# The last head of an mLSTM block: its z units ahead of its weighted values, and one weight split ahead of the squares

## The chip, the cores and the metric

The kernel runs on one core of one Trainium2 chip. The metric is the device time of one execution in microseconds (us); shorter is better. The core has five engines that run side by side, each in the order of its own instructions: TensorE (PE in the profile; its loads of weights are PEld), VectorE (DVE), ScalarE (ACT), GpSimd (POOL), and SyncE (SP), which here only issues DMAs.

## The reference

The block has one layer, 512 positions and 1024 channels. A combined projection gives a Fourier branch (a) and an mLSTM branch (b) of 2048 channels in 4 heads of 512; both are gated, mapped back to 1024 channels, merged and projected once more. What matters here is the end of branch b:

```python
h_cell = h_cell * jax.nn.sigmoid(o_m)                       # per head: 512 positions x 512 channels
h_cell = h_cell * lax.rsqrt(jnp.mean(h_cell * h_cell, axis=-1, keepdims=True) + EPS)
y_b = ((h_cell * hnorm_w[l] + skip_w[l] * x_c) * jax.nn.silu(z_m)) @ w_mlstm[l]
```

## The kernel before

**Split numbers.** Every fp32 weight and activation that TensorE reads is split into a high and a low part: ACT writes the high part (`hi_of`, L90), DVE subtracts it from the source (`lo_of`, L93). A product is three matmuls (`mm3`, L97 high by high, L98 the activation's low part, L99 the weight's low part).

**Weight units.** Weights come in units of 128x1024, fetched by SP into `raw` (3 buffers) and split by `prepare` into `whi` and `wlo` (2 buffers each). `unit()` hands out the oldest split unit and keeps two split ahead in the program's text. A DMA of a new unit is issued with each `prepare`.

**A head.** The loop over `h` makes scores, decay weights and the output gate `so`. Then, for four row tiles t of 128 positions: the weighted values `pv` (12 matmuls in a `wk` bank), `so *= pv` on DVE (L684), the sum of squares on ACT (L686), its root on POOL (L688, L689), and the scaling of `so` on DVE (L690). Then 16 transposes on PE (L700, four per row tile, into one `wk` bank per channel tile d), and for each d on DVE the norm weight and skip (L702), the gate by `sz[d]` (L703), and the split into `u_hi` (tiles `sa`, ACT) and `u_lo` (tiles `sb`, DVE). The four z units of a head (`z_unit`) give `sz`; from the second head on, unit 0 stands ahead of the row tiles and units 1 to 3 behind them.

**Branch b's product.** `u` times `w_mlstm` runs over 16 weight units in two halves of eight. In the first half, units 0 to 3 need `u` of the first two heads alone, units 4 and 5 that of the third, units 6 and 7 that of the last. After units 6 and 7 ACT copies the four sums out (L751). Inside this half lie two calls of `block_sums` for a later stage: POOL fetches `xr`, DVE makes sums `xs` and the low parts `bl` and `tl`, ACT the high parts `bh` and `th`.

**Order.** The text is not the order in which an engine runs. A scheduler in the framework builds one list per engine by a timeline of its own before the kernel runs; `pin` (`keep_in_program_order`) keeps an instruction in the text's order among the pinned ones of its engine. On the chip each engine works off its list strictly in order.

Of the kernel before, what the change touches and what calls it, by code (L numbers as in the profile page):

```python
# [10 lines left out]
AF = mybir.ActivationFunctionType  # L11
ALU = mybir.AluOpType
# [5 lines left out]
NH = 4  # L18
# [7 lines left out]
NU0 = 3  # L26
# [14 lines left out]
def hybrid_block(ctx: ExitStack, tc, xT, x0n, xn, first, units, blocks, vecs, gates, gbias, consts, dft, fnw, out):  # L41
    nc = tc.nc
    te, ve, se, gp = nc.tensor, nc.vector, nc.scalar, nc.gpsimd
# [21 lines left out]
    def tl(tag, shape, dtype=F32, bufs=1, pool=None, shift=0):  # L65
        count[0] += 1
        if pool is None:
            pool = "wide" if tag[:2] in ("sa", "sb") else "gw" if tag in ("gwh", "gwl") else "low" if tag in LOW else "high" if tag in HIGH else "work"


        n = math.prod(shape[1:])
        t = pools[pool][1].tile([shape[0], -(-(n + shift) // 64) * 64], dtype, tag=tag, name=f"{tag}_{count[0]}", bufs=bufs)
        t = t[:, shift : shift + n]
        if len(shape) == 2:
            return t
        names = "abcd"[: len(shape) - 1]
        return t.rearrange(f"p ({' '.join(names)}) -> p {' '.join(names)}", **dict(zip(names, shape[1:])))

    def bank(tag, cols=512, rows=P):
        count[0] += 1  # L80
        return ps.tile([rows, cols], F32, tag=tag, name=f"{tag}_{count[0]}", bufs=4)

    def t2k(dtype=F32, cols=S):
        return tl("t2k", [P, cols], dtype, bufs=3)

    def pin(ins, on=True):
        return tc.keep_in_program_order(ins) if on else ins

    def hi_of(dst, src, scale=1.0, pinned=False):
        pin(se.activation(dst, src, AF.Copy, scale=scale), pinned)  # L90

    def lo_of(dst, src, hi, pinned=False):
        pin(ve.tensor_tensor(out=dst, in0=src, in1=hi.bitcast(F32), op=ALU.subtract), pinned)  # L93

    def mm3(acc, wh, wl, xh, xl, start, stop, pinned=False, group=True):
        skip = {} if group else {"skip_group_check": True}
        pin(te.matmul(acc, wh, xh, start=start, stop=False, **skip), pinned)  # L97
        te.matmul(acc, wh, xl, start=False, stop=False, **skip)  # L98
        te.matmul(acc, wl, xh, start=False, stop=stop, **skip)  # L99
# [25 lines left out]
    def fetch():  # L125
        i = state["raw"]
        if i < nplan:
            raws[i] = tl("raw", [P, 1024], bufs=NRAW)
            if len(plan[i]) == 1:
                w = plan[i][0].shape[1]  # L130
                pin(nc.sync.dma_start(raws[i][:, 0:w], plan[i][0]))
            else:
                for n, src in enumerate(plan[i]):
                    pin(nc.sync.dma_start(raws[i][:, n * S : (n + 1) * S], src))
            state["raw"] += 1

    def raw_unit(i):
        while state["raw"] <= i:
            fetch()
        return raws.pop(i)  # L140

    def prepare():
        i = state["split"]
        r = raw_unit(i)
        extra = i >= first_pair and i % 4 >= 2
        hi = tl("gwh" if extra else "whi", [P, 1024], F32R, bufs=2)
        lo = tl("gwl" if extra else "wlo", [P, 1024], F32R, bufs=2)
        w = 1024 if len(plan[i]) == 2 else plan[i][0].shape[1]
        hi_of(hi[:, 0:w], r[:, 0:w], pinned=i <= NU0 + 2)
        lo_of(lo[:, 0:w], r[:, 0:w], hi[:, 0:w], pinned=i <= NU0 + 2)  # L150
        items.append((hi, lo))
        state["split"] += 1
        fetch()
# [16 lines left out]
    def unit():  # L170
        i = state["split"]
        if state["at"] < len(JOBS) and i >= JOBS[state["at"]]:
            state["at"] += 1
            next_job()
        while len(items) < (4 if "gw" in pools else 2) and state["split"] < nplan:
            prepare()
        return items.pop(0)
# [21 lines left out]
    def col(o):  # L199
        return vc[:, o : o + 1]  # L200
# [46 lines left out]
    for g in range(2):  # L247
        part = []
        for k in range(4):
            sq = tl(f"{('sa', 'sb')[g]}{k}", [P, S])  # L250
# [92 lines left out]
    def first_units():  # L343
        accs = [bank(t) for t in ("acc", "wk", "acc")]
        for n in range(4):
            for i, ((wh, wl), acc) in enumerate(zip(firsts, accs)):
                last = n == 3 and i == 2
                if last:
                    load_gates()
                    prepare()  # L350
                    prepare()
                for k in (2 * n, 2 * n + 1):
                    if last and k == 7:
                        norm_rows()
                    ks = slice(k * P, (k + 1) * P)
                    mm3(acc, wh[:, ks], wl[:, ks], hv(x_hi, k), hv(x_lo, k), k == 0, k == 7, last)
        return accs

    def proj(hooks={}, pinned=False):
        wh, wl = unit()  # L360
        acc = bank("acc")
        for k in range(8):
            if k in hooks:
                hooks[k]()
            ks = slice(k * P, (k + 1) * P)
            mm3(acc, wh[:, ks], wl[:, ks], hv(x_hi, k), hv(x_lo, k), k == 0, k == 7, pinned or any(at <= k for at in hooks))
        return acc

    def evac(dst, acc, func=None, pinned=False):
        pin(ve.tensor_tensor(out=dst, in0=acc, in1=rb, op=ALU.mult), pinned)  # L370
        if func:
            se.activation(dst, dst, func)
# [3 lines left out]
    def new_sz():  # L376
        z2 = [tl(f"sz{n}", [P, 2, S]) for n in range(2)]
        sz.extend(z2[n // 2][:, n % 2, :] for n in range(4))

    def z_unit(d, func=AF.Silu):  # L380
        if not sz:
            new_sz()
        evac(sz[d], proj(), func)
# [42 lines left out]
    def spread_rows(h):  # L426
        for dr in range(2):
            r = 32 * dr + h
            spread[dr] = tl(("mx_r", "em_r")[dr], [P, S])
            pin(nc.sync.dma_start(spread[dr], kept_rows[0][r : r + 1, :].to_broadcast([P, S])))  # L430
        spread[2] = tl("em", [P, S], bufs=2)
        for dr in range(2):
            r = 32 * dr + h
            pin(nc.sync.dma_start(spread[2][64 * dr : 64 * dr + 64], kept_rows[1][r : r + 1, :].to_broadcast([64, S])))
# [58 lines left out]
    for h in range(NH):  # L493
# [100 lines left out]
        so = [so2[t // 2][:, t % 2, :] for t in range(4)]  # L594

        def o_gate():
            for t in range(4):
                se.activation(so[t], ops[t], AF.Sigmoid, scale=rc[:, t : t + 1])
# [42 lines left out]
        r = t2k()  # L641
# [31 lines left out]
        if h < NH - 1:  # L673
            spread_rows(h + 1)
        o_gate()
        if h > 0:
            z_unit(0)
        ss = tl("ss", [P, 4], bufs=2)
        for t in range(4):
            pv = bank("wk")  # L680
            for b in range(4):
                o = (t if t <= b else t + 1) * P
                mm3(pv, whi[b][:, o : o + P], wlo[b][:, o : o + P], vh[b], vl[b], b == 0, b == 3)
            ve.tensor_tensor(out=so[t], in0=pv, in1=so[t], op=ALU.mult)  # L684
            sq = t2k()
            se.activation(sq, so[t], AF.Square, accum_out=ss[:, t : t + 1])  # L686
            r = tl("rr", [P, 1], bufs=4)
            gp.tensor_scalar(out=r, in0=ss[:, t : t + 1], scalar1=1.0 / 512, scalar2=EPS, op0=ALU.mult, op1=ALU.add)  # L688
            gp.tensor_tensor(out=r, in0=r, in1=mhalf, op=ALU.pow)  # L689
            ve.tensor_scalar(out=so[t], in0=so[t], scalar1=r, scalar2=None, op0=ALU.mult)  # L690
        for d in range(4):
            if h > 0 and d > 0:
                z_unit(d)
            c = c0 + d
            se.activation(xc[c], xc[c], AF.Copy, scale=col(V_SK + c))
# [256 lines left out]
    def m_split(key, src):  # L952
        shape = [src.shape[0]] + list(src.shape[1:])
        hi, lo = (tl(f"m{key[0]}{x}{key[1]}", shape, F32R, pool="last") for x in "hl")
        hi_of(hi, src)
        lo_of(lo, src, hi)
        return hi, lo

    mb, mt = {}, {}
    for j in range(8):  # L960
# [19 lines left out]
        else:  # L980
            k = j - 4
            hi, lo = m_split(("c", k), ga)
# [7 lines left out]
            hi, lo = m_split(("d", k), ts)  # L990
# [209 lines left out]
```

## Time and profile before

| | us |
|---|---|
| median of 3 runs | 753.75 (753.0 to 755.37) |
| the profiled execution | 753.18 |
| its span in the trace | 751.4 |
| PE busy in it | 741.6 (99%) |
| DVE, ACT, POOL busy | 529.1, 410.8, 68.0 |

The profiled execution is 0.57 us below the median, and 1.8 us of it lie outside the span. All rows below are of that one execution. A row of a timeline gives the start, the length, the engine, the line with what it writes and reads, and in brackets how long the engine had been idle and what ended that. An instruction's length holds its way through the engine, so that the next one can start before it ends; the step from start to start is what one costs its engine.

### The profile page before, as it was taken

Reading aid. Unit: us, or ns where it says so; the run is one execution under the profiler, and the core shown is the slowest. Engines: PE = TensorE matmul, PEld = TensorE weight load, DVE = VectorE, ACT = ScalarE, POOL = GpSimd, SP = SyncE. Lnnn points to the kernel's source line nnn. Section 1 sums busy time; section 2 is a strip of 40 time slices with the busy share of each in tenths; the row PEclk is TensorE's granted clock in tenths of the full one; section 3 lists DMA queues with packets and bytes.
Section 4 is the critical chain, followed back from the end, with each engine's and each line's share of the span. In section 5 each row is a group of like instructions: output and inputs, shape, how many; then the busy total and the mean of one; then the engine's idle time right before and its main releaser. Section 6 shows DMA issues by size and latency. Waiting matters only on the chain.

```text
span 751.4 us, 10918 instructions
## 1 busy us (share of the span) xinstructions
PE 741.6 (99%) x4127; PEld 640.2 (85%) x4127; DVE 529.1 (70%) x833; ACT 410.8 (55%) x639; POOL 68.0 (9%) x142
## 2 busy tenths in 40 slices
PE   9999999999999999999999999999999999999996
PEld 8888876888888888888888778899999999988885
DVE  6999985785758574757566866257667787556976
ACT  7345465677626772668343443266544587543444
POOL 0001000204100210022100410000010100000002
PEclk9999999999999999999999999999999999999999
DMA  8548865385945489255720794267654466555463
GB/s 293 179 146 232 236 226 140 92 286 134 240 132 223 114 218 298 87 176 132 196 84 29 190 286 137 88 200 220 192 162 151 148 170 196 168 183 152 141 195 115
DMA packets 42243, 131.24 MB, mean 175 GB/s; under 512 B 4880, under 2 KB 5648, under 8 KB 37072
## 3 DMA queue, kind: packets, MB, share of 16 engines
q1 hardware_dynamic: 38288, 106.84, 42.9%
q0 software_dynamic: 3616, 23.33, 15.4%
q8 instruction: 32, 0.52, 0.3%
q10 hardware_dynamic: 288, 0.39, 0.1%
q14 instruction: 19, 0.16, 0.1%
HBM read 128.19 MB, written 44.30 MB: 230 GB/s over the span
## 4 chain that ended last, share of the span: by engine, by line
PE 97%; ACT 1%; DVE 1%; POOL 0%; issue 0%; ACTq 0%; POOLq 0%
PE acc L97 17%; PE acc L99 17%; PE acc L98 17%; PE wk L97 8%; PE wk L98 8%; PE wk L99 8%; PE acc L585 4%; PE acc L584 4%; PE acc L583 4%; PE wk L666 2%; PE acc L1046 1%; PE acc L1048 1%; PE acc L1047 1%; PE wk L304 1%; PE wk L700 1%; PE wk L197 1%
## 5 line engine op out<-in xcount | busy, mean ns | idle before, releaser
L90 ACT ACTIVATE whi<-raw 128x1024 fp32r<-128x1024 f32 (+2 forms) x107 | 108.4, 1018 | 118.1 <-PE acc L98 68.1
L93 DVE TENSOR_TENSOR wlo<-raw,whi 128x1024 fp32r<-128x1024 f32 (+2 forms) x107 | 124.8, 1171 | 66.4 <-ACT whi L90 66.4
L97 PE MATMUL acc<-hhi,whi 128*128 128x512 f32 x240 | 94.6, 394 | 0.0
L98 PE MATMUL acc<-hlo,whi 128*128 128x512 f32 x240 | 93.5, 390 | 0.0
L99 PE MATMUL acc<-hhi,wlo 128*128 128x512 f32 x240 | 93.4, 389 | 0.0
L93 DVE TENSOR_TENSOR gwl<-raw,gwh 128x1024 fp32r<-128x1024 f32 (+1 forms) x39 | 47.1, 1209 | 18.3 <-ACT gwh L90 18.3
L90 ACT ACTIVATE gwh<-raw 128x1024 fp32r<-128x1024 f32 (+1 forms) x39 | 40.9, 1049 | 29.0 <-PE acc L98 10.0
L97 PEld LDWEIGHTS acc<-hhi,whi 128*128 128x128 f32 x240 | 45.2, 188 | 9.5 <-issue 0.2
L98 PEld LDWEIGHTS acc<-hlo,whi 128*128 128x128 f32 x240 | 45.2, 188 | 9.4 <-issue 0.2
L99 PEld LDWEIGHTS acc<-hhi,wlo 128*128 128x128 f32 x240 | 45.0, 188 | 9.4
L584 PE MATMUL acc<-wlo,hhi 128*128 128x512 f32 x128 | 50.5, 395 | 0.0
L585 PE MATMUL acc<-whi,hlo 128*128 128x512 f32 x128 | 50.4, 394 | 0.0
L97 PE MATMUL acc<-sa,whi 128*128 128x512 f32 x128 | 49.3, 392 | 0.9 <-ACT whi L90 0.9
L99 PE MATMUL acc<-sa,wlo 128*128 128x512 f32 x128 | 48.9, 391 | 1.1 <-DVE wlo L93 1.1
L98 PE MATMUL acc<-sb,whi 128*128 128x512 f32 x128 | 49.7, 391 | 0.0
L97 PE MATMUL wk<-vhi,phi 128*128 128x512 f32 x128 | 49.6, 389 | 0.0
L98 PE MATMUL wk<-vlo,phi 128*128 128x512 f32 x128 | 49.6, 389 | 0.0
L99 PE MATMUL wk<-vhi,plo 128*128 128x512 f32 x128 | 48.5, 389 | 0.0
L583 PE MATMUL acc<-whi,hhi 128*128 128x512 f32 x128 | 47.0, 394 | 0.0
L333 DVE SCALAR_TENSOR_TENSOR t2k<-sa,vecs,t2k 128x510 f32<-128x510 f32 (+1 forms) x64 | 44.9, 744 | 0.1
L93 DVE TENSOR_TENSOR vlo<-wk,vhi 128x512 fp32r<-128x512 f32 x32 | 21.0, 682 | 27.5 <-ACT vhi L90 27.5
L99 PEld LDWEIGHTS acc<-sa,wlo 128*128 128x128 f32 x128 | 24.0, 188 | 6.8 <-DVE wlo L93 1.9
(427 smaller groups left out, 1904.1 us busy)
## 6 DMA issues: line engine op xcount, KB each, us to landing
raw<-in_units_dram SPq DMA_DIRECT2D x69, 512.0 KB, 4.2
sum<-in_blocks_dram SPq DMA_DIRECT2D x20, 1024.0 KB, 8.0
raw<-sum SPq DMA_DIRECT2D x64, 256.0 KB, 3.7
raw<-in_blocks_dram SPq DMA_DIRECT2D x48, 256.0 KB, 3.8
sum<-in_blocks_dram POOLq DMA_DIRECT2D x10, 1024.0 KB, 9.7
sum<-sum POOLq DMA_DIRECT2D x10, 1024.0 KB, 9.4
raw<-sum SPq DMA_DIRECT2D x8, 512.0 KB, 4.4
raw<-in_blocks_dram SPq DMA_DIRECT2D x6, 512.0 KB, 4.6
```

The costliest lines, as they stand in the source:

```text
L90: pin(se.activation(dst, src, AF.Copy, scale=scale), pinned)
L93: pin(ve.tensor_tensor(out=dst, in0=src, in1=hi.bitcast(F32), op=ALU.subtract), pinned)
L97: pin(te.matmul(acc, wh, xh, start=start, stop=False, **skip), pinned)
L98: te.matmul(acc, wh, xl, start=False, stop=False, **skip)
L99: te.matmul(acc, wl, xh, start=False, stop=stop, **skip)
L197: te.matmul(junk[:, 0:P], ones, ones, start=True, stop=True)
L304: pin(te.matmul(gate_ps[rows, :], w_gate[j][:, i, :], r, start=n == 0, stop=n == 14, tile_position=(0, 32 * (2 * b + j))), n + b + j > 0)
L333: ve.scalar_tensor_tensor(out=cv[:, o], in0=src[:, s], scalar=cw[k], in1=cv[:, o], op0=ALU.mult, op1=ALU.add)
L583: te.matmul(ops[t], hv(x_hi, k)[:, ts], wh[:, ks], start=k == 0, stop=False)
L584: te.matmul(ops[t], hv(x_hi, k)[:, ts], wl[:, ks], start=False, stop=False)
L585: te.matmul(ops[t], hv(x_lo, k)[:, ts], wh[:, ks], start=False, stop=k == 7)
L666: te.matmul(vp[:, ds], xm[c0 + d][:, b * P : (b + 1) * P], vbf[:, d, :], start=True, stop=True)
```

## The change

In the last head alone, all four z units stand ahead of the row tiles; behind them one `prepare` is called, with its two split instructions pinned; and the products with `pv` and the squares of the four row tiles are pinned too.

```diff
-    def prepare():
+    def prepare(ahead=False):
...
-        hi_of(hi[:, 0:w], r[:, 0:w], pinned=i <= NU0 + 2)
-        lo_of(lo[:, 0:w], r[:, 0:w], hi[:, 0:w], pinned=i <= NU0 + 2)
+        hi_of(hi[:, 0:w], r[:, 0:w], pinned=ahead or i <= NU0 + 2)
+        lo_of(lo[:, 0:w], r[:, 0:w], hi[:, 0:w], pinned=ahead or i <= NU0 + 2)
...
+        last = h == NH - 1
         if h > 0:
-            z_unit(0)
+            for d in range(4 if last else 1):
+                z_unit(d)
+        if last:
+            prepare(True)
         ss = tl("ss", [P, 4], bufs=2)
         for t in range(4):
...
-            ve.tensor_tensor(out=so[t], in0=pv, in1=so[t], op=ALU.mult)
+            pin(ve.tensor_tensor(out=so[t], in0=pv, in1=so[t], op=ALU.mult), last)
             sq = t2k()
-            se.activation(sq, so[t], AF.Square, accum_out=ss[:, t : t + 1])
+            pin(se.activation(sq, so[t], AF.Square, accum_out=ss[:, t : t + 1]), last)
...
         for d in range(4):
-            if h > 0 and d > 0:
+            if 0 < h < NH - 1 and d > 0:
                 z_unit(d)
```

Lines behind L676 move down by four: L684 and L686 become L688 and L690, L690 becomes L694, L700 to L703 become L704 to L707, L723 to L728 become L727 to L732.

What this makes of the lists is seen at three places. **Place 1** is ACT at the row tiles of the last head. `whi_3692` is the high part of branch b's unit 3, `whi_3738` that of unit 4, `phi` are the decay weights that `pv` reads. Before:

```order
L648 ACTIVATE plo_633_3204<-t2k_3199 64x512 x2
L90 ACTIVATE phi_634_3236<-wf_601_3019 128x640
L90 ACTIVATE phi_636_3243<-wf_602_3020 128x640
L90 ACTIVATE phi_638_3250<-wf_603_3021 128x640
L90 ACTIVATE phi_640_3257<-wf_604_3022 128x640
L686 ACTIVATE t2k_3383,ss_3368<-so_616_3127 128x512
L686 ACTIVATE t2k_3403,ss_3368<-so_616_3127 128x512
L686 ACTIVATE t2k_3423,ss_3368<-so_617_3128 128x512
L686 ACTIVATE t2k_3443,ss_3368<-so_617_3128 128x512
L90 ACTIVATE whi_3692<-raw_3634 128x1024
L90 ACTIVATE whi_3738<-raw_3664 128x1024
L90 ACTIVATE bh_712_3618<-xr_3722 128x256
```

After:

```order
L648 ACTIVATE plo_633_3204<-t2k_3199 64x512 x2
L90 ACTIVATE whi_3692<-raw_3471 128x1024
L90 ACTIVATE phi_634_3236<-wf_601_3019 128x640
L90 ACTIVATE phi_636_3243<-wf_602_3020 128x640
L90 ACTIVATE phi_638_3250<-wf_603_3021 128x640
L90 ACTIVATE phi_640_3257<-wf_604_3022 128x640
L690 ACTIVATE t2k_3488,ss_3473<-so_616_3127 128x512
L690 ACTIVATE t2k_3508,ss_3473<-so_616_3127 128x512
L690 ACTIVATE t2k_3528,ss_3473<-so_617_3128 128x512
L690 ACTIVATE t2k_3548,ss_3473<-so_617_3128 128x512
L90 ACTIVATE whi_3738<-raw_3664 128x1024
L90 ACTIVATE bh_715_3624<-xr_3722 128x256
```

The split of unit 3 moved from behind the last square to ahead of the decay weights; that of unit 4 is still behind the last square. Of the 24 matmuls of unit 3, which before all stood behind the first 12 transposes, PE's list now has 16 ahead of the 48 weighted values and 8 among those transposes. The 48 themselves, which took turns over the four row tiles, now go almost tile by tile.

On DVE, at the same place, `wk_3369` to `wk_3429` were the weighted values of row tiles 0 to 3. Before:

```order
L684 TENSOR_TENSOR so_616_3127<-wk_3369,so_616_3127 128x512
L684 TENSOR_TENSOR so_616_3127<-wk_3389,so_616_3127 128x512
L690 TENSOR_SCALAR so_616_3127<-so_616_3127,rr_3385 128x512
L684 TENSOR_TENSOR so_617_3128<-wk_3409,so_617_3128 128x512
L690 TENSOR_SCALAR so_616_3127<-so_616_3127,rr_3405 128x512
L684 TENSOR_TENSOR so_617_3128<-wk_3429,so_617_3128 128x512
L690 TENSOR_SCALAR so_617_3128<-so_617_3128,rr_3425 128x512
L93 TENSOR_TENSOR wlo_3693<-raw_3634,whi_3692 128x1024
```

After, where they are `wk_3474` to `wk_3534`:

```order
L688 TENSOR_TENSOR so_616_3127<-wk_3474,so_616_3127 128x512
L694 TENSOR_SCALAR so_616_3127<-so_616_3127,rr_3490 128x512
L688 TENSOR_TENSOR so_616_3127<-wk_3494,so_616_3127 128x512
L694 TENSOR_SCALAR so_616_3127<-so_616_3127,rr_3510 128x512
L688 TENSOR_TENSOR so_617_3128<-wk_3514,so_617_3128 128x512
L694 TENSOR_SCALAR so_617_3128<-so_617_3128,rr_3530 128x512
L688 TENSOR_TENSOR so_617_3128<-wk_3534,so_617_3128 128x512
L93 TENSOR_TENSOR wlo_3739<-raw_3664,whi_3738 128x1024
```

Each product with `pv` now stands behind the scaling of the tile before it; before, one product stood between.

**Place 2** is PE at the four transposes of row tile 3, the last ones. Before (`acc_3629` is unit 3, `acc_3626` with `whi_3738` the first of unit 4):

```order
L98 MATMUL acc_3629<-sb_446_2312,whi_3692 128x512
L99 MATMUL acc_3629<-sa_445_2311,wlo_3693 128x512
L97 MATMUL acc_3626<-sa_563_2921,whi_3738 128x512
L700 MATMUL wk_3552<-consts_192,so_617_3128 128x128
L700 MATMUL wk_3564<-consts_192,so_617_3128 128x128
L700 MATMUL wk_3576<-consts_192,so_617_3128 128x128
L700 MATMUL wk_3588<-consts_192,so_617_3128 128x128
L98 MATMUL acc_3626<-sb_564_2922,whi_3738 128x512
L99 MATMUL acc_3626<-sa_563_2921,wlo_3739 128x512
```

After (`acc_3633` with `whi_3738` ends unit 4, `acc_3634` begins unit 5):

```order
L98 MATMUL acc_3633<-sb_576_2958,whi_3738 128x512
L99 MATMUL acc_3633<-sa_575_2957,wlo_3739 128x512
L704 MATMUL wk_3558<-consts_192,so_617_3128 128x128
L704 MATMUL wk_3570<-consts_192,so_617_3128 128x128
L704 MATMUL wk_3582<-consts_192,so_617_3128 128x128
L704 MATMUL wk_3594<-consts_192,so_617_3128 128x128
L97 MATMUL acc_3634<-sa_563_2921,whi_3768 128x512
L98 MATMUL acc_3634<-sb_564_2922,whi_3768 128x512
```

The four transposes moved from behind unit 4's first matmul to behind its last. From them to the first matmul that reads `u` of the last head there were 47 matmuls; now there are 24.

**Place 3** is DVE behind those transposes, from the first L702 to the first `sb` of the last head (`sb_691_3561`, now `sb_694_3567`). Before, ten instructions stood ahead of it (one row counts for two):

```order
L702 SCALAR_TENSOR_TENSOR t2k_3557<-wk_3552,vecs_108,sb_138_768 128x512
L702 SCALAR_TENSOR_TENSOR t2k_3569<-wk_3564,vecs_108,sb_140_778 128x512
L702 SCALAR_TENSOR_TENSOR t2k_3581<-wk_3576,vecs_108,sb_142_786 128x512
L93 TENSOR_TENSOR tl_708_3614<-xs_3723,th_704_3610 128x1024
L703 TENSOR_TENSOR t2k_3557<-t2k_3557,sz_657_3331 128x512
L93 TENSOR_TENSOR wlo_3769<-raw_3696,whi_3768 128x1024
L703 TENSOR_TENSOR t2k_3569<-t2k_3569,sz_657_3331 128x512
L723 SCALAR_TENSOR_TENSOR xr_3798<-xr_3798,vecs_108,rb_235 128x512 x2
L703 TENSOR_TENSOR t2k_3581<-t2k_3581,sz_658_3332 128x512
L93 TENSOR_TENSOR sb_691_3561<-t2k_3557,sa_690_3560 128x512
```

After, seventeen do. The three L706, an `xr`, the low part of unit 6 and a second `xr` come first; these are the rest:

```order
L707 TENSOR_TENSOR t2k_3563<-t2k_3563,sz_657_3331 128x512
L727 SCALAR_TENSOR_TENSOR xr_3798<-xr_3798,vecs_108,rb_235 128x512
L707 TENSOR_TENSOR t2k_3575<-t2k_3575,sz_657_3331 128x512
L707 TENSOR_TENSOR t2k_3587<-t2k_3587,sz_658_3332 128x512
L730 TENSOR_TENSOR xs_3723<-xr_3722 128x256
L732 SCALAR_TENSOR_TENSOR xs_3723<-xs_3723,xr_3722 128x256
L93 TENSOR_TENSOR bl_719_3628<-xr_3722,bh_715_3624 128x512
L729 TENSOR_TENSOR xs_3799<-xr_3798 128x256
L93 TENSOR_TENSOR bl_720_3629<-xr_3798,bh_716_3625 128x256
L730 TENSOR_TENSOR xs_3799<-xr_3798 128x256
L93 TENSOR_TENSOR wlo_3845<-raw_3772,whi_3844 128x1024
L93 TENSOR_TENSOR sb_694_3567<-t2k_3563,sa_693_3566 128x512
```

The sums of `block_sums`, which stood ahead of the first L702 or behind the first `sb`, and the low part of unit 7 now lie between the two. On ACT the first `sa` of the last head, before one place behind the split of unit 5, now stands behind that of unit 7 (`whi_3844`).

PE's list is the same up to the first matmuls of branch b's unit 0, the 96 matmuls of the last head's z units among them. SP's list has the same kinds of rows in the same order.

## Rows read from the trace of the kernel before

**Rows 1.** The page: share of the chain that ended last, by engine.

```profile
PE 97%; ACT 1%; DVE 1%; POOL 0%; issue 0%; ACTq 0%; POOLq 0%
```

**Rows 2.** PE's own waits, whole span: us in total, times, longest us.

```profile
PE acc L99 <- DVE wlo L93: 1.1, 2, 0.5
PE acc L97 <- ACT whi L90: 0.9, 2, 0.7
```

**Rows 3.** Timeline of PE at the last head's transposes; start us, us, engine, line, operation.

```profile
415.39 0.39 PE L99 MATMUL wk<-vhi,plo 128*128 128x512 f32 x1
415.62 2.03 PE L700 MATMUL wk<-consts,so 128*128 128x128 f32 x12
418.32 0.50 PE L97 MATMUL acc<-sa,whi 128*128 128x512 f32 x1 [0.67 <-ACT whi L90]
...
419.58 0.50 PE L99 MATMUL acc<-sa,wlo 128*128 128x512 f32 x1 [0.53 <-DVE wlo L93]
419.92 0.39 PE L97 MATMUL acc<-sa,whi 128*128 128x512 f32 x1
```

**Rows 4.** Timeline of PE between the halves of branch b.

```profile
446.73 0.39 PE L99 MATMUL acc<-sa,wlo 128*128 128x512 f32 x1
...
448.99 0.39 PE L97 MATMUL acc<-sa,whi 128*128 128x512 f32 x1
```

**Rows 5.** Timeline of PE at the last four transposes.

```profile
424.02 0.39 PE L97 MATMUL acc<-sa,whi 128*128 128x512 f32 x1
...
424.70 0.39 PE L97 MATMUL acc<-sa,whi 128*128 128x512 f32 x1
424.94 0.60 PE L700 MATMUL wk<-consts,so 128*128 128x128 f32 x4
...
425.60 0.40 PE L99 MATMUL acc<-sa,wlo 128*128 128x512 f32 x1
```

**Rows 6.** Timeline of ACT at the squares of the last head.

```profile
416.60 0.63 ACT L686 ACTIVATE t2k<-so 128x512 f32<-128x512 f32 x1 [1.09 <-DVE so L684]
...
417.23 1.99 ACT L90 ACTIVATE whi<-raw 128x1024 fp32r<-128x1024 f32 x2
```

**Rows 7.** Timeline of DVE at the row tiles.

```profile
410.83 0.69 DVE L684 TENSOR_TENSOR so<-wk,so 128x512 f32<-128x512 f32 x1 [5.41 <-PE wk L99]
...
413.23 0.49 DVE L690 TENSOR_SCALAR so<-so,rr 128x512 f32<-128x512 f32 x1
...
415.82 0.69 DVE L684 TENSOR_TENSOR so<-wk,so 128x512 f32<-128x512 f32 x1 [0.52 <-PE wk L99]
...
418.30 1.23 DVE L93 TENSOR_TENSOR wlo<-raw,whi 128x1024 fp32r<-128x1024 f32 x1 [1.36 <-ACT whi L90]
```

**Rows 8.** Timeline of DVE from the first L702 of the last head on.

```profile
425.24 2.07 DVE L702 SCALAR_TENSOR_TENSOR t2k<-wk,vecs,sb 128x512 f32<-128x512 f32 x3
...
430.70 1.41 DVE L723 SCALAR_TENSOR_TENSOR xr<-xr,vecs,rb 128x512 f32<-128x512 f32 x2
...
432.63 0.68 DVE L93 TENSOR_TENSOR sb<-t2k,sa 128x512 fp32r<-128x512 f32 x1
433.23 1.22 DVE L93 TENSOR_TENSOR wlo<-raw,whi 128x1024 fp32r<-128x1024 f32 x1
...
437.84 0.42 DVE L728 SCALAR_TENSOR_TENSOR xs<-xs,xr 128x256 f32<-128x256 f32 x1
438.17 1.22 DVE L93 TENSOR_TENSOR wlo<-raw,whi 128x1024 fp32r<-128x1024 f32 x1
```

**Rows 9.** Timeline of POOL: the four fetches of `xr`.

```profile
416.53 2.31 POOL L722 DMA_DIRECT2D xr<-in_xT_dram  x4
```

**Rows 10.** All eight fetches of `xr`, from issue to landing.

```profile
DMA to landing us min/median/max: 3.3/4.0/13.3
```

**Rows 11.** Stretches: us, busy us (instructions) of PE, PEld, DVE, ACT, POOL, granted clock, DMA.

```profile
416.00:420.00 4.00, 2.67 (x14) 1.49 (x13) 2.30 (x4) 2.62 (x4) 3.73 (x7) 1.00 0.53 163
749.00:750.00 1.00, 0.00 (x0) 0.00 (x0) 0.00 (x0) 0.00 (x0) 0.00 (x0) 1.00 0.86 322
```

## The prediction

> **What bounds the kernel now.** I read the chain of waits first: 97% of it is PE [rows 1], so time is won or lost only where PE stands still. The list of PE's waits says how often that is: apart from the start, twice for a high part and twice for a low part of a weight unit [rows 2]. PE's timeline gives the places. The first is the end of the last head [rows 3]: from 415.62 to 419.92, 4.30 us, PE does 12 transposes and 3 matmuls. A matmul costs 0.227 us (424.02 to 424.70 are three), and four transposes cost 425.60 - 424.94 - 0.227 = 0.43, so 0.108 each [rows 5]. That is 1.30 + 0.68 of work; **2.32 us is standing still**. The second place lies between the halves of branch b [rows 4]: 446.73 to 448.99 holds four matmuls, 0.91 of 2.26 us, so 1.35 are lost. In both, PE waits for the split of the next weight unit, on ACT and then on DVE. The change touches the first place alone. Its most possible gain is thus 2.32 us, 0.31% of 753.75; about 0.3% is what a measurement of this kernel can tell from no change.
>
> **The z units and the pins.** PE's 96 matmuls of the last head's z units keep their place, so moving them in the text costs and gives PE nothing. The only trace is that the split of unit 1 comes a few places later on ACT and DVE. Were the unit not ready, the loss would be at most one split, 1.07 from high to low part [rows 6, 7] and 1.28 from there to PE [rows 3, 7]; at the least it is nothing. I take nothing, because unit 0's matmuls lie in front of it. The pins are not instructions and cost nothing by themselves; SP's list is unchanged, so no DMA is issued past another one.
>
> **The early split of unit 3: 2.32 us gained, part of it given back.** The split no longer waits behind the last square (416.60 and then 417.23 [rows 6]), so 16 of unit 3's matmuls can run ahead of the weighted values and 8 among the transposes. What is late next is unit 4, whose high part is still behind the last square. I follow that chain in the time of the trace of before.
> - PE: the last weighted value started at 415.39 [rows 3]; 16 matmuls more make it 415.39 + 3.63 = 419.02. Then come 12 transposes and 8 matmuls, so PE reaches unit 4 at 419.02 + 0.227 + 1.30 + 1.82 = 422.37.
> - DVE: a product with pv starts 0.43 after the last matmul's start (415.39 to 415.82 [rows 3, 7]), and its own scaling starts 2.40 later (410.83 to 413.23, by way of ACT and POOL [rows 7]) and costs 0.40 (0.49 long, and a step is 0.08 to 0.09 shorter than a length: 432.63 to 433.23 for 0.68 [rows 8]). Since each product now stands behind the scaling of the tile before it, four tiles are 2.80 apart, while PE delivers one every 12 x 0.227 = 2.72. Tile 0 ends 33 matmuls before the last one, at 411.53; so its product starts at 411.96 and tile 3's at 411.96 + 3 x 2.80 = 420.36, and not at 419.45, when PE would allow it.
> - ACT and on: square 0.78 later (415.82 to 416.60), high part 0.63 after that (to 417.23), PE 1.09 after that (to 418.32), low part 1.07 after the high part's start (to 418.30), its first matmul 1.28 after that (to 419.58; the 1.23 of its length and 0.05) [rows 3, 6, 7]. So the high part starts at 421.77, PE at 422.86, and the first matmul with the low part at 424.12.
>
> PE waits 0.49 for the first. Four matmuls run by the high part alone; the one behind a wait costs 0.34 instead of 0.227 (419.58 to 419.92 [rows 3]), so they end at 423.88 and PE waits 0.24 again. With 0.11 for each restart, **0.95 us is given back**.
>
> **The later transposes: a new wait.** The transposes of tile 3 follow unit 4's other 20 matmuls: 424.12 + 0.34 + 19 x 0.227 = 428.77. The first L706 follows 0.30 later (424.94 to 425.24 [rows 5, 8]), at 429.07; DVE has by then done the low parts of units 4 and 5, if `xr` has landed. It is fetched behind tile 2's root, at about 420; the issues take 2.31 and the quickest landing 3.3 [rows 9, 10], while DVE wants it at about 424.4.
>
> From here DVE has 17 instructions to do before the first low part of the last head's u. Their price comes from the stretch of before that holds almost the same ones without a pause, 425.24 to 438.17, 12.93 us [rows 8]. It has one L702 (0.66), one `tl` (1.13, the size of a `wlo`) and three `sb` (0.60 each) more, and one `xr` (0.66) and one `xs` (0.33) fewer: 12.93 - 0.66 - 1.13 - 1.80 + 0.66 + 0.33 = 10.33. The low part starts at 439.40, and PE can read it 0.73 later (its 0.68 and the same 0.05 as above), at 440.13.
>
> PE has 4 transposes and 24 matmuls to do meanwhile: it is done with unit 5 at 428.77 + 0.43 + 5.45 = 434.65. Two waits follow.
> - The first u's high part (`sa`) stands on ACT behind unit 7's split, which needs the buffer that unit 5's last matmul but one frees: 434.65 - 0.45 + 0.43 = 434.63 (a release at the price of rows 7). Its step is 0.95 (two are 1.99 long [rows 6]), and `sa` takes 0.63 and 0.05: PE starts at 436.26, a wait of 1.61.
> - Four matmuls read high parts alone, to 437.28. Then the low part is wanted, which comes at 440.13: 2.85 more.
>
> With two restarts this is **4.68 us lost**. It would vanish only if PE had other work there, and its list has none. The rest of u follows close on the first low part, with PE's next reads 32 matmuls on, so I add no third wait. The joint at 446 has the same rows in the same order and keeps its 1.35.
>
> **The sum.** -2.32 + 0.95 + 4.68 = +3.3 us. The profiled execution took 753.18, 0.57 below the median; it becomes 756.5, and the median 753.75 becomes **757.0**, 0.44% slower.
>
> **Rivals.**
> - *The gain without the new wait* (8%). For it speaks that the old wait does go. It needs u's low part by 437.28; DVE would have to do its 17 instructions in 7.5 us. It decides at a new loss of 2.32 - 0.95 = 1.37: below that the kernel is not slower. With none, 753.75 - 1.37 = 752.4. Against it stands a DVE without a pause in the very stretch.
> - *Half the new wait* (12%). The price of the 17 instructions is a sum of steps, and tile 3's transposes could come up to 0.95 sooner if unit 4 does not wait. With half of 4.68: 753.75 + 1.0 = 754.7.
> - *The xr fetch lands late* (6%). The longest of the eight landings is 13.3 [rows 10]. DVE stops at L727 and with it everything behind: from 424.4 to 433.3, of which the pause before 429.07 hides some 2; about 6 us more, 763. Against it: the four are issued close together and in the same place of POOL's list as before.
> - *The clock falls after the new wait* (4%). In a stretch with 1.33 of 4 us idle the granted clock was 1.00, the upper level of 2.4 GHz, and in 749 to 750, with PE idle throughout, it still was [rows 11]. At 1.2 GHz a matmul takes 0.45 instead of 0.227; for half of the 44 that are left of units 6 and 7 this is 5 us, 762. The Trainium skill, page "TensorE: Matmul & The Clock Gate", section "Why this matters for your kernels", asks to leave no long idle gaps between bursts of matmuls, since one sends the clock back to half; by that rule this change risks both losses. The trace disagrees so far as its own idle stretches go, none of which had matmuls behind it at half the clock.
> - *The change doesn't do what it says*: the split does stand ahead of the squares in ACT's list, so this has no chance of its own; of the z units it is true.
>
> **How the numbers follow.** The forecast has 70%; it spans some 0.8 us each way, since four terms are differences of starts rounded to 0.01 that rest on a single execution, and since runs of before differ by 2.4 us. The range takes in the half wait: 754.4 to 758.8, and leaves out the full gain, the late fetch and the clock. Slower by over 0.3% (above 756.0): nine tenths of the forecast's 70%, and the late fetch and the clock, 72%. Within 0.3%: the rest of the forecast, the half wait and most of the gain, 22%. Faster: 6%.
>
> **What would show it.** In the trace after: no PE wait at the first 12 transposes; a wait of about 0.5 for unit 4's high part and 0.2 for its low part; then, some 12 us later, waits of about 1.6 for `sa` on ACT and 2.8 for `sb` on DVE, with DVE busy throughout from the first L706; then 1.35 at the joint as before. It is wrong if PE waits for `sb` under 1.4 us in all, or if another wait, for `xr` or `raw`, stands there.

## The result, and the profile after

The median rose from 753.74 us to **758.66 us** (six executions each, 752.96 to 755.37 and 758.09 to 760.5): a ratio of 1.0067, with an interval of 1.0052 to 1.0082. The change costs 4.9 us. The profiled execution of the changed kernel took 760.5, its span is 758.7. It falls 1.4 us behind within its first 25 us, at its first loads and long before the change, and keeps that: its first product with `pv` starts at 413.40 where the prediction has 411.96. All times of this trace below stand 1.44 later than those of the prediction for that reason.

PE's waits now, whole span (us in total, times, longest us), against [rows 2]:

```profile
PE acc L97 <- ACT sa L90: 2.1, 1, 2.1
PE acc L98 <- DVE sb L93: 2.0, 1, 2.0
...
PE acc L97 <- ACT whi L90: 0.9, 3, 0.3
PE acc L99 <- DVE wlo L93: 0.5, 1, 0.5
```

Two waits of about 2 us that were not there before now lead the list, for the two halves of the last head's u. PE's timeline at the last head's transposes, against [rows 3] (start us, us, engine, line, operation; in brackets idle and releaser):

```profile
420.46 0.39 PE L99 MATMUL wk<-vhi,plo 128*128 128x512 f32 x1
420.69 0.27 PE L704 MATMUL wk<-consts,so 128*128 128x128 f32 x1
...
422.52 0.39 PE L99 MATMUL acc<-sa,wlo 128*128 128x512 f32 x1
422.75 1.25 PE L704 MATMUL wk<-consts,so 128*128 128x128 f32 x10
424.34 0.50 PE L97 MATMUL acc<-sa,whi 128*128 128x512 f32 x1 [0.33 <-ACT whi L90]
...
425.14 0.40 PE L98 MATMUL acc<-sb,whi 128*128 128x512 f32 x1
425.60 0.50 PE L99 MATMUL acc<-sa,wlo 128*128 128x512 f32 x1
```

The 2.32 us of standing still behind the last weighted value are gone. Instead unit 4 is waited for: 424.34 - 422.75 less ten transposes at 0.108 is 0.51, and 425.60 - 425.14 - 0.227 is 0.23. Ten microseconds on comes the large loss:

```profile
435.96 0.39 PE L99 MATMUL acc<-sa,wlo 128*128 128x512 f32 x1
438.45 1.20 PE L97 MATMUL acc<-sa,whi 128*128 128x512 f32 x4 [2.10 <-ACT sa L90]
441.64 0.80 PE L98 MATMUL acc<-sb,whi 128*128 128x512 f32 x1 [2.00 <-DVE sb L93]
442.24 0.63 PE L99 MATMUL acc<-sa,wlo 128*128 128x512 f32 x1
442.67 0.63 PE L97 MATMUL acc<-sa,whi 128*128 128x512 f32 x1
...
446.93 0.43 PE L98 MATMUL acc<-sb,whi 128*128 128x512 f32 x1
447.20 0.40 PE L99 MATMUL acc<-sa,wlo 128*128 128x512 f32 x1
```

From start to start PE loses 438.45 - 435.96 - 0.227 = 2.26 for `sa`. Four matmuls (0.91) later it loses 441.64 - 438.45 - 0.91 = 2.28 for `sb`, of which 0.11 is the restart behind the first wait and 2.17 the wait. Then something follows that no wait explains: from 442.24 to 446.93 eleven steps take 4.69 us, 0.426 each instead of 0.227. The stretches show why (us, busy us (instructions) of PE, PEld, DVE, ACT, POOL, then the granted clock, DMA):

```profile
436.00:440.00 4.00, 1.54 (x6) 0.67 (x4) 4.00 (x10) 3.14 (x5) 0.00 (x0) 1.00 1.01 258
440.00:447.00 7.00, 5.36 (x13) 4.20 (x14) 7.00 (x12) 2.29 (x3) 2.37 (x5) 0.51 0.95 374
447.00:452.00 5.00, 5.00 (x23) 4.10 (x22) 1.53 (x2) 0.46 (x1) 0.76 (x1) 1.00 0.91 218
```

The granted clock went to half, 1.2 GHz, during the second wait and came back at 447. PE counts as busy for 5.36 of those 7 us, but its matmuls step at half their pace. Over the page's 40 slices it is one digit, PEclk 8 in the slice where PE falls to 7:

```profile
PE   9999999999999999999999979999999999999996
...
PEclk9999999999999999999999989999999999999998
```

DVE explains the second wait, against [rows 8]; it works without a pause from the first L706 to the first low part of u:

```profile
430.58 2.07 DVE L706 SCALAR_TENSOR_TENSOR t2k<-wk,vecs,sb 128x512 f32<-128x512 f32 x3 [1.32 <-PE wk L704]
...
439.77 1.21 DVE L93 TENSOR_TENSOR wlo<-raw,whi 128x1024 fp32r<-128x1024 f32 x1
440.91 0.68 DVE L93 TENSOR_TENSOR sb<-t2k,sa 128x512 fp32r<-128x512 f32 x1
```

440.91 - 430.58 is 10.33. ACT explains the first: `sa` stands behind unit 7's split, and that one waited for its weights.

```profile
436.81 1.06 ACT L90 ACTIVATE whi<-raw 128x1024 fp32r<-128x1024 f32 x1 [1.25 <-DMA raw<-in_units_dram]
437.78 0.61 ACT L90 ACTIVATE sa<-t2k 128x512 fp32r<-128x512 f32 x1
```

### The profile page after: what moved, and what is told of

Same layout as the page of the kernel before. It is cut to its first block, busy times and chain, and to the rows that moved or that the text cites. A ratio compares the mean times of both kernels' runs of the same rounds, so it can differ in the third digit from the quotient of the medians.

```text
span 758.7 us, 10917 instructions
## 1 busy us (share of the span) xinstructions
PE 745.2 (98%) x4127; PEld 641.9 (85%) x4127; DVE 528.7 (70%) x833; ACT 410.6 (54%) x639; POOL 67.3 (9%) x142
## 4 chain that ended last, share of the span: by engine, by line
PE 92%; DVE 3%; ACT 2%; DMA 2%; POOL 1%; issue 1%; ACTq 0%; DVEq 0%; POOLq 0%
PE acc L99 16%; PE acc L97 16%; PE acc L98 16%; PE wk L98 7%; PE wk L97 7%; PE wk L99 7%; PE acc L584 4%; PE acc L585 4%; PE acc L583 4%; PE wk L666 2%; DMA raw<-in_first_dram 2%; PE acc L1052 1%; PE acc L1050 1%; PE acc L1051 1%; PE wk L304 1%; PE wk L704 1%
## 5 line engine op out<-in xcount | busy, mean ns | idle before, releaser
L97 PEld LDWEIGHTS acc<-sa,whi 128*128 128x128 f32 x128 | 24.5, 192 | 8.8 <-ACT sa L90 2.5
```

## Experiments

The theory: the early split moves the last transposes late, and so DVE's block sums come to stand between them and u's first low part; PE runs dry there, and the clock falls behind the two waits. Rivals: the z units or the pins cost the time; the queue on DVE is not what PE waits for; the slow matmuls have another cause than the waits. The executions of the kernel before beside these runs had medians of 753.25, 753.21 and 753.30, so ratios are what is compared.

### Zero matmuls for both waits

The changed kernel with eight matmuls by a block of zeros ahead of the first matmul that reads the last head's u, and eight behind it. They add zero to the sums.

```diff
+    zz = tl("zz", [P, P], F32R, pool="late")
+    hi_of(zz, ident, scale=0.0)
...
+                if q == 0 and n == 6 and k == 0:
+                    for _ in range(8):
+                        te.matmul(accs[j], zz, u_hi[11], start=False, stop=False)
+                    te.matmul(accs[j], wh[:, ks], u_hi[c], start=False, stop=False)
+                    for _ in range(8):
+                        te.matmul(accs[j], zz, u_hi[11], start=False, stop=False)
```

> The changed kernel with 16 more matmuls on TensorE by a block of zeros, which add nothing to a sum: 8 ahead of the first matmul on the last head's u, 8 behind it, where TensorE stands still twice for about 2.2 us. Each costs 0.227 us, 1.8 us in each wait, so the data come no later. Theory (the two waits cost 3.3 us net as predicted, and the rest of the loss is the clock that falls to 0.50 behind them): the waits on sa and sb nearly vanish from the profile, the granted clock stays 1.00 there (mean 0.999), and although 3.6 us of work are added the kernel gets faster than the changed one by the clock's 1.6 to 2.6 us and some 0.4 us of restarts: 756.0 to 756.7, ratio 1.003 to 1.004. Rival (the clock is a by-product, and the rest is data that come late, such as the raw unit that landed 1.25 us late): 758.2 to 758.7, ratio 1.006 to 1.007.

Measured: 756.05 us, ratio 1.0040 (1.0027 to 1.0052): with 3.6 us of work added, it is 2.6 us faster than the changed kernel (2.0 by the ratios). Only the second eight ran inside a wait, at 436.79 to 438.60, behind the first matmul on u. The first eight read tiles that are ready early, and the scheduler put them around the last four transposes, at 428.84 to 431.12 (the next run has the same order and shows the rows); they make PE reach u 1.8 us later. The same stretches:

```profile
436.00:440.00 4.00, 3.64 (x17) 2.71 (x16) 4.00 (x9) 3.12 (x5) 1.11 (x2) 1.00 0.97 307
440.00:446.00 6.00, 6.00 (x27) 4.95 (x27) 5.47 (x9) 1.41 (x2) 0.84 (x3) 1.00 0.85 342
```

The clock stays at 1.00 and all matmuls behind the place step 0.227 again. So the half clock goes with PE standing still there: the matmuls read the same data, and the DMAs are about as busy (0.97 and 0.85 here, 1.01 and 0.95 in the changed kernel, 1.01 at the full clock in the next run). Not all of the gain is the clock's: the added lines also changed the lists of DVE and ACT. Of the 17 instructions an `xr` now stands ahead of the first L706 and the low part of unit 7 behind `sb`, an `xs` and a `bl` have come in, and `sb` comes 9.47 us behind the first L706 instead of 10.33; on ACT the first `sa` now stands ahead of the split of unit 7.

### The first eight zero matmuls alone

```diff
+                if q == 0 and n == 6 and k == 0:
+                    for _ in range(8):
+                        te.matmul(accs[j], zz, u_hi[11], start=False, stop=False)
```

> The changed kernel with eight matmuls by zero weights ahead of the first one that reads u of the last head, and none between the first and the one by its low part. They are 1.82 us of work in the first of the two new waits, 2.3 us long, so about 0.5 of that wait stays. The second wait ends when DVE has written the low part, which the fill does not move: it should stay near 2.2 us. If the clock fell because two waits stood close together, one alone leaves it at 1.00 and the time falls by the 1.6 us that the clock cost in the median: 757.0, in the trace 12 matmuls behind the wait 0.227 apart. If one wait of 2.2 us is enough, the clock falls as before and the time stays at 758.7.

Measured: 756.07 us, ratio 1.0043 (1.0029 to 1.0057). None of the eight ran in the first wait: two stand ahead of the last four transposes and six behind them. The wait for `sa` was gone altogether, since PE reaches u 1.8 us later and ACT writes `sa` (435.30) ahead of unit 7's split (436.46). One wait for unit 7's high part and the one for `sb` were left:

```profile
428.71 0.62 PE L755 MATMUL acc<-sa,zz 128*128 128x512 f32 x2
429.16 0.60 PE L704 MATMUL wk<-consts,so 128*128 128x128 f32 x4
429.52 1.64 PE L755 MATMUL acc<-sa,zz 128*128 128x512 f32 x6
...
437.57 0.73 PE L97 MATMUL acc<-sa,whi 128*128 128x512 f32 x2 [0.52 <-ACT whi L90]
439.67 0.50 PE L757 MATMUL acc<-sb,whi 128*128 128x512 f32 x1 [1.37 <-DVE sb L93]
```
```profile
436.00:440.00 4.00, 2.11 (x8) 1.14 (x7) 4.00 (x9) 3.05 (x4) 1.17 (x2) 1.00 1.01 313
440.00:446.00 6.00, 6.00 (x28) 4.93 (x27) 5.47 (x9) 1.54 (x2) 0.92 (x2) 1.00 0.84 347
```

The clock stays up, with PE idle for 1.89 of these 4 us. The second wait came out shorter than expected (1.4 instead of 2.2, since here too `sb` was 9.47 behind the first L706), so whether one wait of 2.2 would do stays open. The time is that of the run before it, though eight matmuls fewer are added: those eight ran where PE otherwise waits for DVE, and are free. The first eight are not quite: the two ahead of the transposes make these start 0.45 us later.

### The block sums moved to the second half

The changed kernel with all four calls of `block_sums` in the second half of branch b.

```diff
-SUMS_AT = ((0, 3), (0, 5), (1, 1), (1, 3))
+SUMS_AT = ((1, 0), (1, 1), (1, 2), (1, 3))
```

> The changed kernel with all four block sums of the later stage moved from the first half of branch b to its second half, so that DVE has no xr, xs, bl and tl among the instructions between the transposes and the first low part of u. Theory (the new wait is DVE's queue): its 17 instructions lose 3 xr, 4 xs and 2 bl, 4.2 us, ahead of the first sb; the waits on sa and sb are gone, the clock stays up, and what is left is the gain of 2.3 less the 0.95 at unit 4: 753.7 - 1.35 = 752.4, ratio 0.998. Rival (the later transposes alone make u late, 24 matmuls of cover instead of 47): a wait on sb of 1 us or more stays, 753.5 or above.

Measured: 752.3 us, ratio 0.9988 (0.9980 to 0.9997). PE's waits:

```profile
PE acc L97 <- ACT whi L90: 1.3, 4, 0.5
...
PE acc L99 <- DVE wlo L93: 0.5, 1, 0.5
```

`sa` and `sb` are gone from the list: the new wait was what stood ahead of u in the other engines' lists. `sb` now comes 4.92 us behind the first L706 (434.08 - 429.16) instead of 10.33. Of the 5.41 less, the nine instructions of the block sums are some 4.3; the low part of unit 7, which now stands behind `sb` as well, is 1.1. The time is the one expected, but what of it is the change's only the run of the moved sums alone, below, can tell.

### The parts of the change one by one

The z units alone ahead; no early split and no pins:

```diff
-        if last:
-            prepare(True)
...
-            pin(ve.tensor_tensor(out=so[t], in0=pv, in1=so[t], op=ALU.mult), last)
+            ve.tensor_tensor(out=so[t], in0=pv, in1=so[t], op=ALU.mult)
...
-            pin(se.activation(sq, so[t], AF.Square, accum_out=ss[:, t : t + 1]), last)
+            se.activation(sq, so[t], AF.Square, accum_out=ss[:, t : t + 1])
```

> Only the first part of the change: the last head's z units ahead of its row tiles, without the extra split and without pins. Theory: PE's list of the last head and branch b is the one of before, so 753.7, ratio 1.000, with the old waits of 0.67 and 0.53 at unit 3. Rival (the early z units are what moves PE's work): waits on sa and sb as in the changed kernel, 757 or more.

Measured: 753.33 us, ratio 1.0004 (0.9995 to 1.0013), with the waits of [rows 2]. The z units alone change nothing that this can tell.

z units and pins, without the early split (only the first two lines of that diff):

> The change without the extra split: z units ahead and the four products and squares pinned. Theory: unit 3's split stays behind the last square, and the pinned products stand one behind the other's scaling on DVE, 2.80 us apart, so that the old wait grows: about 1.3 us slower than before, 755.0, ratio 1.0017; no wait on sa or sb. Rival (the pins are harmless): 753.7.

Measured: 755.5 us, ratio 1.0038 (1.0026 to 1.0050). Transposes now wait for the scaling (L692) and the product (L686) ahead of them, and unit 3's high part comes later; then the clock falls here too, which the expectation had left out. PE's timeline and its stretches:

```profile
415.64 0.38 PE L702 MATMUL wk<-consts,so 128*128 128x128 f32 x2
416.58 0.44 PE L702 MATMUL wk<-consts,so 128*128 128x128 f32 x2 [0.56 <-DVE so L692]
417.18 0.44 PE L702 MATMUL wk<-consts,so 128*128 128x128 f32 x2 [0.16 <-DVE so L686]
418.94 0.76 PE L97 MATMUL acc<-sa,whi 128*128 128x512 f32 x1 [1.32 <-ACT whi L90]
```
```profile
414.00:418.00 4.00, 2.89 (x14) 1.82 (x13) 1.42 (x3) 1.51 (x5) 2.63 (x6) 1.00 0.13 27
418.00:422.00 4.00, 2.99 (x6) 1.95 (x7) 3.09 (x5) 2.36 (x4) 1.16 (x3) 0.63 0.85 283
```

From start to start PE stood still for 2.65 of the 3.30 us from 415.64 to 418.94, with six transposes between. The kernel before, which keeps 1.00 [rows 3, 11], stood still for 1.40 of the 2.70 us from 415.62 to 418.32, with twelve: the waits of 0.67 and 0.53 in brackets leave out those inside its row of transposes.

The early split and the z units, without the pins on the products and the squares (only the last four lines of that diff; the split itself keeps its pins, other than the expectation says):

> The changed kernel without the pins: the four z units stand ahead and one unit is split ahead of the squares, but the products, the squares and the split are not pinned. In DVE's list there are still 16 instructions between the last L706 and the first low part of the last head's u (the four xr, the block sums and two low parts of units among them). If the early split alone makes the new wait, the waits at u add up to 4.0 to 5.0 us, the clock falls behind them as in the changed kernel, and the time is 757.5 to 759.5. If the pins make it, the waits at u are under 1 us and the time is 752.5 to 753.5.

Measured: 758.95 us, ratio 1.0076 (1.0056 to 1.0097), and the picture of the changed kernel:

```profile
PE acc L97 <- ACT sa L90: 2.3, 1, 2.3
PE acc L98 <- DVE sb L93: 2.0, 1, 2.0
```
```profile
434.00:440.00 6.00, 1.65 (x6) 0.70 (x5) 6.00 (x12) 4.09 (x6) 1.17 (x2) 0.88 1.01 358
440.00:445.00 5.00, 4.99 (x12) 3.93 (x13) 4.48 (x8) 1.34 (x2) 0.72 (x2) 0.50 0.62 253
```

So the early split brings the two waits and the half clock, without the pins on products and squares. Between the last L706 and `sb` the trace has 15 instructions, two of the four `xr` among them, and `sb` comes 10.60 us behind the first L706. The pins have a price where the split does not move, and none here.

### Two units split ahead

The changed kernel with units 3 and 4 split ahead of the squares.

```diff
             prepare(True)
+            prepare(True)
```

> The changed kernel with a second pinned split: units 3 and 4 are both split ahead of the squares, the block sums stay where they are. In DVE's list 10 instructions then stand between the last L706 (here L707) and the first low part of the last head's u instead of 16 behind the L706: bl, a wlo, an xs and some sums fall behind it. By the theory (the new wait is DVE's queue) the wait at unit 4, 0.74 in the trace of the changed kernel, goes and the two waits of 4.65 shrink to 1.0 to 2.0, too short for the clock: 753.5 to 754.5, the same as before. If the queue is not what the new wait comes from, 4.65 us and the clock's loss stay and only 0.95 goes: 757.7.

Measured: 754.02 us, ratio 1.0010 (1.0001 to 1.0019). Unit 4's waits are gone. `sb` now comes 7.24 us behind the first such product (435.67 - 428.43) instead of 10.33:

```profile
428.43 2.07 DVE L707 SCALAR_TENSOR_TENSOR t2k<-wk,vecs,sb 128x512 f32<-128x512 f32 x3 [1.04 <-PE wk L705]
...
435.67 0.69 DVE L93 TENSOR_TENSOR sb<-t2k,sa 128x512 fp32r<-128x512 f32 x1
```

From the last such product to `sb` there are 8 instructions instead of 14; the expectation counts two more in both. PE waits for `sb` for 0.5 us, and 0.5 and 0.3 for the high and the low part of unit 7; the clock stays up over the whole span (mean 0.999). The price of the new wait follows DVE's queue.

### The block sums moved, without the change

The kernel before, with the `SUMS_AT` of the third experiment and nothing else.

> The kernel before with the four calls of the block sums all in branch b's second half, nothing else. If the change itself gives its 1.4 us and the moved sums only keep it from being lost, this is 753.3 to 753.7, no different from the kernel before, with the old waits at the last head's transposes (2.32 us). If the moved sums free ACT and DVE at the joint between the halves, the 1.35 us that PE stands there go, and this is 752.3, as good as both together; then the change is worth nothing beside it.

Measured: 751.98 us, ratio 0.9985 (0.9976 to 0.9994), no worse than with the change (0.9988). The old waits stay, and those of the joint [rows 4] are gone from the list:

```profile
PE acc L97 <- ACT whi L90: 0.7, 1, 0.7
PE acc L99 <- DVE wlo L93: 0.5, 1, 0.5
```

ACT's timeline at the joint tells why: in this list PE ends unit 6 four microseconds before unit 7, so the first copy starts at 441.59 and the split for the second half right behind it.

```profile
441.59 0.60 ACT L751 ACTIVATE yb<-acc 128x512 f32<-128x512 f32 x1 [3.88 <-PE acc L99]
442.09 1.06 ACT L90 ACTIVATE whi<-raw 128x1024 fp32r<-128x1024 f32 x1
```

With the change and the moved sums both units end together:

```profile
444.97 0.60 ACT L755 ACTIVATE yb<-acc 128x512 f32<-128x512 f32 x1 [4.97 <-PE acc L99]
445.46 1.05 ACT L90 ACTIVATE whi<-raw 128x1024 fp32r<-128x1024 f32 x1
```

That split is late, and the joint's waits are back: beside the moved sums, the change gives at one place what it takes at the other. This is the second case of the expectation: the change is worth nothing beside the moved sums.

### All three

The changed kernel with the sums moved, two units split ahead, and two of the four copies at the joint on DVE.

```diff
-SUMS_AT = ((0, 3), (0, 5), (1, 1), (1, 3))
+SUMS_AT = ((1, 0), (1, 1), (1, 2), (1, 3))
...
             prepare(True)
+            prepare(True)
...
-                    se.activation(mg[-1], accs[j], AF.Copy)
+                    if q == 0 and j < 2:
+                        ve.tensor_copy(mg[-1], accs[j])
+                    else:
+                        se.activation(mg[-1], accs[j], AF.Copy)
```

> The changed kernel with the block sums in the second half, a second pinned split ahead of the squares, and two of the four copies at the end of the first half on DVE instead of ACT. In the run with the sums alone moved 752.3 was measured; PE's gaps left there were 0.62 at unit 4 (0.606 and 0.463 from start to start for 0.227), 0.35 at u's first matmul, and 1.13 at the joint (0.663 and 0.920). By the theory that each PE wait is the split that stands behind other work on its engine, the 0.62 goes and 0.3 of the joint: 751.4. If the second split only moves the wait on to unit 5 or to u, it stays at 752.3 or rises.

Measured: **750.68 us**, ratio 0.9965 (0.9953 to 0.9977), faster than both kernels and 0.7 us better than expected. The 0.35 at u's first matmul went too, which the expectation had listed and not counted, and so did the restarts of 0.11 behind that wait and the two at unit 4; the joint gave 0.2 instead of 0.3. No run has the moved sums and the copies on DVE without the change, so what the change itself is worth here stays open. Behind the start, PE's list of waits has one row for this part of the kernel:

```profile
PE acc L99 <- DVE wlo L93: 0.5, 1, 0.5
```

## Why the prediction came out as it did

The prediction, slower at 757.0 with 754.4 to 758.8, had the direction, the place and the mechanism of the waits. That the time lies inside its range, 0.14 below the upper end, is partly luck: the range was drawn to leave the fall of the clock out, and the clock fell. It fits because the fall cost half of what the rival gave it; the profiled execution, 5.9 slower than that of before, lies beyond the 5.05 that the range allows. By the prediction's own terms, in the profiled execution:

| term | forecast | measured |
|---|---|---|
| waits at the first transposes | -2.32 | gone: -2.32 |
| unit 4: high part, low part | 0.49, 0.24 | 0.51, 0.23 |
| from the first L706 to `sb` on DVE | 10.33 | 10.33 |
| wait for `sa`, for `sb` | 1.61, 2.85 | 2.26, 2.17 |
| both, with two restarts | 4.68 | 4.65 |
| the joint, from start to start | 2.26 | 2.26 |
| the clock behind the waits | not in the sum | 2.5 |

- **The gain and what unit 4 takes back** were right. The products with `pv` start 2.81, 2.79 and 2.84 apart (413.40, 416.21, 419.00, 421.84) where 2.80 was forecast: a step taken from start to start in the trace of before could be carried into a new order on DVE.
- **The new wait** was right in its sum and wrong in its parts. The step that failed is the release of ACT's split of unit 7: the prediction let it wait for a buffer; it waited 1.25 us for its fetch. (A wait for `raw` there was one of the prediction's signs of being wrong; it is ACT's here, not PE's own.) Three fetches of weights in that stretch took 11.1 us to land (median), 3.6 over the whole kernel, beside the `xr` and `sum` fetches; no run here shows what slowed them. That made the first wait 0.65 longer and the second 0.68 shorter, because `sb` hung on DVE and on nothing else. The end of the second wait alone sets the time.
- **The z units and the pins** cost nothing here, as forecast; the pins alone, without the split, cost 2.3 us (z units and pins alone).
- **The clock** is the step that was mis-sized: it was a rival with 4%, set against the forecast as another case at 762, where it comes *with* the forecast and adds to it. Eleven matmuls lost 0.20 each and the restart lost 0.26 more, 2.5 us, half the price in the rival's text, which let 22 matmuls run slow. The rows it was judged by [rows 11] were 1.33 us of idle time in 4, and 749 to 750, in the idle end of the trace, where the clock "still was" at 1.00. That reading stopped one row short. PE's last matmul starts at 744.51, and 5.2 us after it ended the trace of before does show the fall, with no matmuls behind it:

```profile
750.00:751.00 1.00, 0.00 (x0) 0.00 (x0) 0.00 (x0) 0.00 (x0) 0.00 (x0) 0.51 0.00 0
```

In the changed kernel PE was idle for 4.4 of the 5.7 us from 435.96 to 441.64, and ahead of its end the trace of before has no stretch that comes near that.
- -2.32 + 0.97 + 4.65 + 2.5 = 5.8; the profiled executions, less the late start, differ by 760.5 - 1.44 - 753.18 = 5.9, the medians by 4.9. Executions of one kernel differ by about 2.4, so the last microsecond stays open.
- **The chances** have a slip: nine tenths of 70%, and 6% and 4%, make 73%, not 72%.

The Trainium skill, page "TensorE: Matmul & The Clock Gate", section "Why this matters for your kernels", asks to leave no long idle gaps between bursts of matmuls. This trace agrees that standing still sends the clock to half (0.51 in 440 to 447), and shows that no single gap need be long: the longest here was 2.3 us, with the z units and pins alone 1.3.

## What to carry to other kernels

Splitting a weight early is worth what PE then waits for next, and that is read by counting what the other engines have queued between the last thing PE gives them and the next thing it needs. When a change leaves two waits of some 2 us close together on TensorE, add the price of matmuls at half the clock behind them to the sum, not to the list of rivals. Work that is due later (here block sums, due in the next stage) should leave the queue of an engine that PE is about to wait for: moving it brought 0.15% by one line, and 0.35% together with the change, a second early split and two copies moved to DVE.

## What the runs showed of the hardware

The clock fell behind two waits of 2.3 and 2.2 us with four matmuls between them, and came back at 447, 5.3 us after matmuls had started again without a pause; in between a matmul of 512 columns stepped 0.426 us instead of 0.227. With the z units and pins alone it fell behind 2.65 us of standing still in 3.30, six transposes between (0.63 in 418 to 422), and 1.40 in 2.70 at the same place in the kernel before did not bring it down; nor did waits of 0.5 and 1.4 us with two matmuls between (the first eight zero matmuls alone). With eight matmuls by zeros inside the second wait and eight around the last transposes PE was idle for 0.36 of 4 us, and the clock stayed at 1.00.
